# Both token sublayers in a new order: plain x scaled early, x^T's second half split ahead, quadrant sums on VectorE, more low parts by transfers

## The chip, the cores and the metric

The kernel runs on one core of a Trainium2 chip as one program. The metric is the device time of one execution in microseconds: 1684.34, the median of three runs (1683.64 to 1687.1). The engines are named as the profile names them: PE (TensorE's matmuls) and PEld (its weight loads), DVE (VectorE), ACT (ScalarE), POOL (GpSimd) and SP (SyncE, which here only issues transfers).

## The reference

Two layers over 512 tokens of width 1024, in fp32. Each has a token sublayer and a channel sublayer:

```python
for i in range(DEPTH):                       # DEPTH = 2
    proj = x @ w_in[i]
    q_na, k_na, v_na, q_r, k_r, v_r, g_r, gate_a, gate_b = jnp.split(proj, IN_SPLITS, axis=-1)
    ya = neighbourhood_attention(q_na, k_na, v_na, na_rpb[i])          # 8 heads of 64
    yb = bidirectional_retention(q_r, k_r, v_r, g_r, decay_f[i], decay_b[i])   # 4 heads, group norm, silu gate
    merged = sigmoid(gate_a) * (ya @ w_branch_a[i]) + sigmoid(gate_b) * (yb @ w_branch_b[i])
    x = layer_norm(DEEPNORM_ALPHA * x + merged @ w_out[i], ln1_g[i], ln1_b[i])
    ffn = conv_glu_ffn(x, w_up[i], conv_w[i], conv_b[i], w_down[i])
    ple = sigmoid(x @ w_ple_gate[i]) * (p[i] @ w_ple_proj[i])
    x = layer_norm(DEEPNORM_ALPHA * x + ffn + ple, ln2_g[i], ln2_b[i])
```

## The kernel before

**Three products for one.** PE multiplies a reduced-precision type. So each fp32 operand is split in a high part `hi`, a cast by ACT, and a low part `lo = src - hi`, a subtraction by DVE (`split`), and each product is hi*hi + hi*lo + lo*hi in fp32. Weights arrive as 128 x 1024 tiles of 512 KB and are split the same way. A few plain weight tiles are "sent": ACT writes -hi into `lo`, and a transfer issued by POOL accumulates the raw weights onto it out of memory, so that DVE has no part in it (`SENT`, seven tiles).

**Seven products for eight.** The large weight matrices are cut into 2 x 2 quadrants and multiplied in seven block products with the names a, c, t1, d, t2, t3, t4. The t's need sums of quadrants: of weights, by a transfer that accumulates onto a raw tile (rawa, rawt), and of x, on DVE and ACT (`quad_sums`; tiles s, s1, s2). `ON_CHIP` names sums that are instead added on the chip from a tile that is there anyway (the quadrant d, rawd); before, that is block 2's t2 in layer 0, added by POOL. In the token sublayer, blocks 0 to 3 of the input projection (values, gates), and the block 4 (the retention's output projection, "branch b", tiles yw and yq, products u, v, w) are of this kind; heads' q and k (`q0`..`k3`, `nq0`..`nk3`) and the output projection are plain tiles.

**The order.** `Stream` holds all weight tiles in the order of use; `get` prepares (splits) up to `DEEP` items ahead, held to three pairs of hi and lo that lie ready, and loads `LOOK` = 3 further. The order of the token sublayer is a list of names: `VG[l]`, its opening, then `FILL[l]`, between whose items the attention and retention heads are spread at slots (`RET_AT`, `NA_AT`). Side jobs hang on steps of the opening through `at_key` (tables, decay logs, x^T's second half, sums: `TABLES_AT`, `REST_AT`). Then `bb` runs branch b, merges (tiles M, sa), splits the transposed sum (mt), multiplies it by w_out (products gn) and ends with layer norm 1 of `xn`, the plain residual x, tile by tile; `ba` is branch a.

**x of layer 1.** Layer 0's last layer norm leaves its normalised rows R without scale and shift; they are stored to `scr` in memory (L1788, L1815). In layer 1's `bb`, `plain_x` loads them as xn and multiplies by lng and adds lnb (L1126, L1127), four tiles each, on DVE.

**The start.** x^T arrives in two halves of columns (xf, two tiles each), and is split by `first_half` and `second_half`. The second also issues the decay vector `dl` and `zd`, and runs `decay_logs`, the logs of the retention's decay rates, on DVE and ACT. In layer 0's `VG` block 3's a (`3a`) comes first, then `nq0`.

Of the kernel before, what the change touches and what calls it, by code (L numbers as in the profile page):

```python
# [14 lines left out]
P = 128  # L15
# [17 lines left out]
SENT = (('k3', 'q2'), ('k2', 'k3', 'nk2', 'nq3', 'q1'))  # L33
# [4 lines left out]
FILL = (('2c', '3t2', '3d', 'nk1', 'vn', '3t3', '3t4', '2t1', 'nk2', '2t2', '2d', '2t3', '0a', 'nq2', 'k2', '0t1', '2t4', '0t2', '0d', '0t3', '1a', 'q0',  # L38
# [9 lines left out]
OUT_PREP = ((0, 1, 1, 1), (0, 1, 1, 1))  # L48
# [3 lines left out]
VG = (('p0', 'p1', '3a', 'nq0', 'nk3', 'nq3', '3c', '3t1', 'nk0', '2a', 'nq1'), ('3a', '2a', '2c', '3c', '3t1', 'nq0', 'nk1', 'nk0', '3t2'))  # L52

XN_AT = (6, 6)
M_AT = (1, 5)
TABLES_AT = (0, 6)
REST_AT = (1, 1, 1, 1, 7, 8)
PEND_AT = (1, 3)

PG = ("a", "c", "up", "t1", "up", "t2", "up", "d", "up", "t3", "up", "t4")  # L60
PG_HELD = ("t1", "t2", "t3", "t4")
PG_EARLY = "a"
# [14 lines left out]
S_AT = ("up0", "t1", "t2", "up1")  # L77
# [3 lines left out]
VG_EARLY = 'd'  # L81
VG_HELD = (('0c', '0t2', '1a', '1c', '1t2', '1t4', '2a', '2t4', '3t1', '3t2'),
 ('0a', '0c', '0d', '0t3', '1c', '1t4', '2a', '2c', '2t1', '2t3', '3a', '3c', '3d', '3t1', '3t2', '3t3'))
ON_CHIP = (('', '', 't2', ''), ('', '', '', ''))
BB_HELD = (('t2',), ('c', 'd', 't1', 't2', 't4'))
BB_EARLY = ('a', 'a')
RC_ACT = ((0, 2, 3, 5, 6, 7), (3, 4, 6))
# [38 lines left out]
def trunk(tc, wpack, x_nat, x_tr, head, p_tr, rpb, decay, ln_par, ln_col, conv, cos_t, sin_t, dist, xi_d, zd, ident_d, out):  # L126
# [4 lines left out]
    with ExitStack() as es:  # L131
# [49 lines left out]
        class Item:  # L181
# [7 lines left out]
            def __init__(self, kind, src, width, pool=None, plus=None, own=None):  # L189
                self.kind, self.src, self.width, self.pool, self.plus, self.own = kind, src, width, pool, plus, own  # L190
                self.raw = self.hl = None
                self.nxt = self.early = self.block = self.other = None

                self.sent = False

        def block_items(pos, held, early, onchip=""):

            out = []
            prev = {}
            for kind, src, plus in (("a", "a", None), ("c", "c", None), ("t1", None, "b"), ("t2", None, "d"),  # L200
                                    ("d", "d", None), ("t3", "b", "d"), ("t4", None, "c")):
                for j in range(2):
# [6 lines left out]
                    if kind == "t3":  # L209
                        [o for o in out if o.kind == early][j].early = it  # L210
# [1738 lines left out]
```

## Time and profile before

| | before |
|---|---|
| median of three runs | 1684.34 us (1683.64 to 1687.1) |
| the profiled execution | 1689.1 us, its span 1687.3 us |
| mean granted clock of PE | 0.997 |
| bytes read, written | 295.37 MB, 26.21 MB |
| hi casts of one 128 x 1024 tile, ACT | 1.05 us |

The span runs from the first instruction to the last. A row of the timeline gives start, length (us), engine, line, operation, tiles (out<-in), and in brackets the time for which its engine stood idle before it and what released it. Matmuls of PE overlap, so that a row of 0.39 us is followed by the next after 0.23. Where the kernel records instructions and issues them itself in a set order, as in the first 75 us, all of them show the line of that helper, L109. Most of DVE's time is low parts (`lo<-raw,hi` and its kin), most of ACT's is casts.

### The profile page before, as it was taken

The page shows a single profiled execution, that of the slowest core. Times are in us where ns is not written, and L with a number is a line of the kernel's source. Part 1 is how long each engine was busy: PE and PEld are TensorE (multiplying, and loading weights), DVE is VectorE, ACT ScalarE, POOL GpSimd, SP SyncE. Part 2 cuts the span into 40 slices and gives each one's busy share as a digit, 9 for nine tenths or more (in the row PEclk, how much of TensorE's full clock was granted, in tenths as well). Part 3 has the DMA queues.
Part 4 walks back from the last instruction along what each step waited for, and adds up shares of the span by engine and source line. Part 5 has one row for each costly group of instructions (what it writes and reads, how often), then busy time and mean ns, then how long its engine had stood idle before and what let it go on. Part 6 is the DMA issues. An engine that isn't in the chain of part 4 may idle for free.

```text
span 1687.3 us, 22720 instructions
## 1 busy us (share of the span) xinstructions
PE 1656.4 (98%) x8391; PEld 1399.0 (83%) x8391; DVE 1314.1 (78%) x2019; ACT 996.3 (59%) x1520; POOL 232.2 (14%) x277
## 2 busy tenths in 40 slices
PE   8999999999999999999999999999999999999997
PEld 6788888887888889789888888888877888898986
DVE  5847688979687867959976676788897887588598
ACT  5858876635266636546486888464533664474462
POOL 0102101110111111111111011010202111111112
PEclk9999999999999999999999999999999999999999
DMA  8857846556774788697686669544767767787874
GB/s 298 223 169 200 206 98 171 168 161 175 233 208 157 174 272 211 157 258 198 182 239 191 187 163 237 163 100 126 187 205 231 218 180 205 220 202 186 249 194 81
DMA packets 94719, 324.13 MB, mean 192 GB/s; under 512 B 10896, under 2 KB 11408, under 8 KB 94608
## 3 DMA queue, kind: packets, MB, share of 16 engines
q0 software_dynamic: 33840, 121.13, 36.7%
q1 hardware_dynamic: 60768, 201.55, 33.0%
q8 instruction: 66, 1.08, 0.2%
q14 instruction: 45, 0.37, 0.1%
HBM read 295.37 MB, written 26.21 MB: 191 GB/s over the span
## 4 chain that ended last, share of the span: by engine, by line
PE 59%; DVE 14%; issue 13%; DMA 8%; ACT 3%; POOL 1%; SPq 0%; DVEq 0%; POOLq 0%; ACTq 0%
PE u L435 4%; PE u L436 4%; PE u L434 4%; DMA rawa<-in_wpack 4%; PE gt L434 4%; PE gt L435 4%; PE gt L436 4%; PE gt L109 3%; DVE lo L179 3%; PE gn L436 3%; PE gn L434 3%; PE gn L435 3%; PE v L434 3%; PE v L436 3%; PE v L435 3%
## 5 line engine op out<-in xcount | busy, mean ns | idle before, releaser
L179 DVE TENSOR_TENSOR lo<-raw,hi 128x1024 fp32r<-128x1024 f32 (+1 forms) x156 | 188.9, 1217 | 97.6 <-ACT hi L178 97.0
L178 ACT CAST hi<-raw 128x1024 fp32r<-128x1024 f32 (+1 forms) x156 | 161.6, 1045 | 151.1 <-DMA raw<-in_wpack 57.7
L179 DVE TENSOR_TENSOR lo<-rawa,hi 128x1024 fp32r<-128x1024 f32 (+1 forms) x151 | 180.3, 1201 | 64.0 <-ACT hi L178 63.0
L178 ACT CAST hi<-rawa 128x1024 fp32r<-128x1024 f32 (+1 forms) x151 | 154.4, 1032 | 125.9 <-DMA rawa<-in_wpack 49.7
L342 POOL DMA_DIRECT2D rawa<-in_wpack x111 | 98.2, 885 | 624.9 <-DVE lo L179 481.7
L109 PE MATMUL gt<-x1t,hi 128*128 128x512 f32 x384 | 118.3, 389 | 0.0
L434 PE MATMUL gt<-x1t,hi 128*128 128x512 f32 x256 | 99.7, 390 | 0.0
L435 PE MATMUL gt<-x1t,hi 128*128 128x512 f32 x256 | 99.7, 390 | 0.0
L436 PE MATMUL gt<-x1t,lo 128*128 128x512 f32 x256 | 99.6, 389 | 0.0
L434 PE MATMUL gt<-xt,hi 128*128 128x512 f32 x216 | 84.7, 392 | 1.1 <-DVE t L886 0.7
L109 PEld LDWEIGHTS gt<-x1t,hi 128*128 128x128 f32 x384 | 72.1, 188 | 15.0
L435 PE MATMUL gt<-xt,hi 128*128 128x512 f32 x216 | 84.2, 390 | 0.0
L436 PE MATMUL gt<-xt,lo 128*128 128x512 f32 x216 | 84.2, 390 | 0.0
L342 POOL DMA_DIRECT2D rawt<-in_wpack x38 | 33.8, 890 | 309.7 <-DMA rawt<-in_wpack 116.2
L109 PE MATMUL gt<-x1t,lo 128*128 128x512 f32 x192 | 74.9, 390 | 0.1
L109 DVE TENSOR_TENSOR lo<-raw,hi 128x1024 fp32r<-128x1024 f32 (+1 forms) x46 | 54.5, 1197 | 5.2 <-ACT hi L109 4.9
L436 PEld LDWEIGHTS gt<-x1t,lo 128*128 128x128 f32 x256 | 48.1, 188 | 10.1
L434 PEld LDWEIGHTS gt<-x1t,hi 128*128 128x128 f32 x256 | 48.1, 188 | 9.6
L435 PEld LDWEIGHTS gt<-x1t,hi 128*128 128x128 f32 x256 | 48.1, 188 | 9.5
L179 DVE TENSOR_TENSOR lo<-rawt,hi 128x1024 fp32r<-128x1024 f32 (+1 forms) x36 | 42.8, 1193 | 14.8 <-ACT hi L178 14.6
L436 PE MATMUL gn<-hi,mt 128*128 128x512 f32 x128 | 49.3, 391 | 1.5 <-DVE mt L179 1.5
L435 PE MATMUL u<-lo,s 128*128 128x512 f32 x128 | 50.4, 394 | 0.0
(499 smaller groups left out, 5128.6 us busy)
## 6 DMA issues: line engine op xcount, KB each, us to landing
raw<-in_wpack SPq DMA_DIRECT2D x205, 512.0 KB, 4.8
rawa<-in_wpack POOLq DMA_DIRECT2D x124, 512.0 KB, 7.1
rawa<-in_wpack SPq DMA_DIRECT2D x42, 512.0 KB, 6.2
rawt<-in_wpack SPq DMA_DIRECT2D x42, 512.0 KB, 6.0
rawt<-in_wpack POOLq DMA_DIRECT2D x42, 512.0 KB, 7.6
s<-s_scr POOLq DMA_DIRECT2D x32, 512.0 KB, 11.7
s_scr<-s POOLq DMA_DIRECT2D x16, 512.0 KB, 5.1
r_scr<-pp SPq DMA_DIRECT2D x8, 512.0 KB, 10.6
```

What stands on the lines that cost most here:

```text
L109: r = f(*a, **k)
L178: nc.scalar.copy(hi, src)
L179: nc.vector.tensor_sub(lo, src, _f(hi))
L342: nc.gpsimd.dma_start(it.raw[:, :w], wpack[l, c][:, o:o + w], accum_op=ALU.add)
L434: nc.tensor.matmul(ps, lh, rh, start=start, stop=False, skip_group_check=more)
L435: nc.tensor.matmul(ps, lh, rl, start=False, stop=False, skip_group_check=more)
L436: nc.tensor.matmul(ps, ll, rh, start=False, stop=stop, skip_group_check=more)
```

## The change

It reorders both token sublayers' lists and moves six things.

- **x early.** `early_x` multiplies R by lng, adds lnb and stores to `scr` in layer 1's opening (`PX_AT` gives the steps); layer 0's end no longer stores R, and `plain_x` only loads.
- **Start.** `dl` and `zd` are issued behind raw_11; the second half's split runs as a hook within the first `a`, between its product and its copies. The opening of layer 0 is now 3a, 3c, nk1, nq1, 2a, nk3, nq0, 3t1.
- **Quadrant sums.** Blocks 0 and 1 (t2 and t3) in layer 0, block 1's t3 and block 3's t2 in layer 1 and branch b's t2 in both are added by DVE from the raw tile of d (or of the like) when the tile is prepared; POOL adds none.
- **Low parts.** Nine plain tiles in place of seven, both tiles of branch b's d in each layer, and three and one tiles of the output projection are sent: 17 in all.
- **Group norm.** In layer 0 the last scale of the four heads (yb) is done by ACT; more heads' softmax scales (S) are done by DVE (`RC_ACT`).
- The ple projection's stores, tables and sums move to other steps. The switches for the channel sublayer that come with it (`D_CHIP`, `U_CHIP`, `PG_CHIP`, `M_SENT`, `UBP`, `PG_CHORE`) are all off.

```diff
-SENT = (('k3', 'q2'), ('k2', 'k3', 'nk2', 'nq3', 'q1'))
+SENT = (('k0', 'nk2', 'nq2', 'q0', 'q2', 'q3'), ('k2', 'nq1', 'q3'))
...
-FILL = (('2c', '3t2', '3d', 'nk1', 'vn', '3t3', '3t4', '2t1', 'nk2', '2t2', '2d', '2t3', '0a', 'nq2', 'k2', '0t1', '2t4', '0t2', '0d', '0t3', '1a', 'q0',
-  'k0', '0t4', '1t1', '0c', 'k1', 'q1', '1t2', '1d', 'k3', 'q3', '1t3', '1c', 'q2', '1t4', 'ba'),
...
+FILL = (('nk0', 'nq3', '3t2', '3d', 'vn', '3t3', 'nq2', 'nk2', '2c', '3t4', '2t1', '2d', '2t2', '0a', '2t3', '2t4', '0t1', '0t2', '0d', '0t3', 'k2', 'k3',
+  '1a', '0t4', '1t1', '1c', 'k0', '1d', 'k1', 'q0', '1t2', 'q1', '0c', 'q2', '1t3', 'q3', '1t4', 'ba'),
...
-RET_AT = ((33, 32, 38, 37), (31, 38, 36, 39))
-NA_AT = ((10, 13, 13, 16, 18, 19, 20, 23), (6, 9, 9, 10, 11, 11, 17, 20))
+RET_AT = ((36, 36, 38, 40), (37, 39, 38, 40))
+NA_AT = ((9, 9, 13, 14, 15, 19, 21, 24), (7, 8, 10, 12, 13, 14, 20, 21))
...
-VG = (('p0', 'p1', '3a', 'nq0', 'nk3', 'nq3', '3c', '3t1', 'nk0', '2a', 'nq1'), ('3a', '2a', '2c', '3c', '3t1', 'nq0', 'nk1', 'nk0', '3t2'))
+VG = (('p0', 'p1', '3a', '3c', 'nk1', 'nq1', '2a', 'nk3', 'nq0', '3t1'), ('2a', '3a', '3c', 'nq1', 'nq2', '3t1', 'nq0', 'nk1'))
...
+PX_AT = (4, 15, 16, 17, 18, 18, 38, 40, 41, 42)
+GN_ACT = ((0, 1, 2, 3), ())
+BSENT = (('4d',), ('4d',))
+OUT_SENT = ((1, 4, 5), (6,))
...
+BB_CHIP = ('t2', 't2')
...
-ON_CHIP = (('', '', 't2', ''), ('', '', '', ''))
+ON_CHIP = (('t2 t3', 't2 t3', '', ''), ('', 't3', '', 't2'))
...
-RC_ACT = ((0, 2, 3, 5, 6, 7), (3, 4, 6))
+RC_ACT = ((0, 2, 5), (3, 5))
...
             def add(self, it):
                 if it.other is not None:
-                    if it.other.raw is None:
-                        self.fetch(it.other)
-                    nc.gpsimd.tensor_tensor(it.raw, it.raw, it.other.raw, ALU.add)
                     return
...
+                    if it.other is not None:
+                        o = it.other
+                        if o.raw is None:
+                            self.fetch(o)
+                        nc.vector.tensor_add(it.raw[:, :it.width], it.raw[:, :it.width], o.raw[:, :it.width])
...
+        NDL = DEPTH * 8
+        lgs = cp.tile([P, NDL], F32, name="lgs")
+        dl = cp.tile([P, NDL], F32, name="dl_0")
+        nc.sync.dma_start(dl, decay.to_broadcast([P, NDL]))
+        nc.sync.dma_start(zd_sb, zd)
         for kp in range(2):
             x_load(1, kp)
...
             ws.load(11)
-            nc.sync.dma_start(dl, decay.to_broadcast([P, NDL]))
-            nc.sync.dma_start(zd_sb, zd)
...
                         product(kind, st["u"], True)
+                        while hooks:
+                            next(hooks.pop(0))
                         st["p1"] = copies(st["u"], "p1")
...
-                        nc.vector.tensor_scalar_mul(y, y, r[:, i:i + 1])
+                        if h in GN_ACT[l]:
+                            nc.scalar.activation(y, y, AF.Copy, scale=r[:, i:i + 1])
+                        else:
+                            nc.vector.tensor_scalar_mul(y, y, r[:, i:i + 1])
...
                     xn.append(z)
-                    if l:
-                        nc.vector.tensor_mul(z, z, g)
-                        nc.vector.tensor_add(z, z, b)
+
+            def early_x():
+
+                g, b = ln_consts(l - 1, 1)
+                yield
+                for t in range(5):
+                    if t < 4:
+                        nc.vector.tensor_mul(RX[t], RX[t], g)
+                        yield
+                    if t:
+                        nc.sync.dma_start(scr[(t - 1) * P:t * P, :], RX[t - 1])
+                    if t < 4:
+                        nc.vector.tensor_add(RX[t], RX[t], b)
+                    yield
...
                             norm(i)
-                            nc.sync.dma_start(scr[i * P:(i + 1) * P, :], R[i])
```

**SP's queue at the start.** hd is the first product's data, xf the four tiles of x^T, raw and rawa weight tiles, dl the decay vector. Before, from the eighth transfer:

```order
L109 DMA raw_11_123<-in_wpack 128x1024
L109 DMA xf_12_125<-in_x_tr 128x1024
L109 DMA xf_13_127<-in_x_tr 128x1024
L109 DMA raw_24_158<-in_wpack 128x1024
L1698 DMA gb_7332<-in_ln_col 128x16
L109 DMA raw_35_204<-in_wpack 128x1024
L109 DMA cos_sb_88<-in_cos_t 128x512
...
L109 DMA ident_84<-in_ident 128x128
L109 DMA raw_40_249<-in_wpack 128x1024
L109 DMA raw_43_267<-in_wpack 128x1024
L109 DMA dl_0_140<-in_decay 128x16
```

and now:

```order
L125 DMA raw_11_123<-in_wpack 128x1024
L125 DMA dl_0_126<-in_decay 128x16
L125 DMA zd_sb_87<-in_zd 128x4
L125 DMA xf_12_129<-in_x_tr 128x1024
L125 DMA xf_13_131<-in_x_tr 128x1024
L125 DMA raw_26_164<-in_wpack 128x1024
L665 DMA B_115_656<-in_rpb 128x512
L665 DMA B_116_658<-in_rpb 128x512
L125 DMA raw_27_166<-in_wpack 128x1024
```

The decay vector and zd stand ahead of the second half of x^T now, in place of behind the fourteenth large transfer, and the attention's bias tables B between two weight tiles.

**DVE at the start.** lo is a weight tile's low part, xt a split of x^T (xf 12 and 13 are its second half), qn and kl parts of attention heads, p1 a block product's copy. Before:

```order
L109 TENSOR_TENSOR lo_42_264<-raw_24_158,hi_41_263 128x1024
L109 TENSOR_TENSOR xt_0_106<-xf_12_125,xt_0_106 128x2x256
L109 TENSOR_TENSOR xt_0_106<-xf_13_127,xt_0_106 128x2x256
L109 TENSOR_TENSOR xt_0_106<-xf_12_125,xt_0_106 128x2x256
L109 TENSOR_TENSOR xt_0_106<-xf_13_127,xt_0_106 128x2x256
L109 TENSOR_SCALAR dl_1_299<-dl_0_140 128x16
L109 TENSOR_TENSOR dl_1_299<-dl_1_299,dl_0_140 128x16
...
L109 TENSOR_TENSOR lo_48_321<-raw_35_204,hi_47_320 128x1024
L109 TENSOR_TENSOR qn_51_352<-qs_50_349,qn_51_352 64x512 x2
L109 TENSOR_TENSOR lo_53_362<-raw_40_249,hi_52_361 128x1024
```

and now:

```order
L125 TENSOR_TENSOR lo_45_272<-raw_27_166,hi_44_271 128x1024
L125 TENSOR_TENSOR xt_0_106<-xf_12_129,xt_0_106 128x2x256
L125 TENSOR_TENSOR xt_0_106<-xf_13_131,xt_0_106 128x2x256
L125 TENSOR_TENSOR xt_0_106<-xf_12_129,xt_0_106 128x2x256
L125 TENSOR_TENSOR xt_0_106<-xf_13_131,xt_0_106 128x2x256
L125 TENSOR_TENSOR lo_54_310<-raw_38_212,hi_53_309 128x1024
L125 TENSOR_TENSOR lo_56_326<-rawa_43_257,hi_55_325 128x1024
...
L125 TENSOR_TENSOR kl_60_376<-gt_58_350,kn_59_375 64x512 x4
L125 TENSOR_TENSOR lo_62_386<-rawa_46_275,hi_61_385 128x1024
L125 TENSOR_TENSOR qn_65_418<-qs_64_415,qn_65_418 64x512 x2
...
L125 TENSOR_TENSOR s_81_475<-s1_79_472,s_80_474 128x512
L125 TENSOR_SCALAR dl_1_480<-dl_0_126 128x16
```

The decay logs (dl) stood ahead of the sixth weight tile's low part; they now come fifteen rows later, behind the work on the next weight tiles, heads and x's first sums.

**DVE in layer 1, around the merge.** M and sa are the merge, mt the split of its transpose, xn the plain x, lng and lnb the layer norm's scale and shift of the layer before. Before, behind sa:

```order
L1126 TENSOR_TENSOR xn_2013_11366<-xn_2013_11366,lng_2011_11362 128x1024
L1127 TENSOR_TENSOR xn_2013_11366<-xn_2013_11366,lnb_2012_11363 128x1024
L1126 TENSOR_TENSOR xn_2014_11370<-xn_2014_11370,lng_2011_11362 128x1024
L1126 TENSOR_TENSOR xn_2015_11374<-xn_2015_11374,lng_2011_11362 128x1024
L1127 TENSOR_TENSOR xn_2014_11370<-xn_2014_11370,lnb_2012_11363 128x1024
L1127 TENSOR_TENSOR xn_2015_11374<-xn_2015_11374,lnb_2012_11363 128x1024
L1126 TENSOR_TENSOR xn_2016_11378<-xn_2016_11378,lng_2011_11362 128x1024
L179 TENSOR_TENSOR mt_2022_11422<-tr_2020_11416,mt_2021_11421 128x4x128
L1127 TENSOR_TENSOR xn_2016_11378<-xn_2016_11378,lnb_2012_11363 128x1024
L179 TENSOR_TENSOR mt_2022_11422<-tr_2023_11425,mt_2021_11421 128x4x128
L179 TENSOR_TENSOR mt_2026_11438<-tr_2024_11432,mt_2025_11437 128x4x128
L179 TENSOR_TENSOR mt_2026_11438<-tr_2027_11441,mt_2025_11437 128x4x128
```

and now, from sa on:

```order
L1250 TENSOR_TENSOR sa_1868_10606<-sa_1868_10606,M_1987_11259 128x512
L1250 TENSOR_TENSOR sa_1869_10608<-sa_1869_10608,M_1988_11261 128x512
L195 TENSOR_TENSOR mt_2019_11425<-tr_2017_11419,mt_2018_11424 128x4x128
L195 TENSOR_TENSOR mt_2019_11425<-tr_2020_11428,mt_2018_11424 128x4x128
L195 TENSOR_TENSOR mt_2023_11441<-tr_2021_11435,mt_2022_11440 128x4x128
L195 TENSOR_TENSOR mt_2023_11441<-tr_2024_11444,mt_2022_11440 128x4x128
L195 TENSOR_TENSOR lo_2033_11461<-raw_2002_11335,hi_2032_11460 128x1024
L195 TENSOR_TENSOR lo_2035_11465<-raw_2013_11383,hi_2034_11464 128x1024
L195 TENSOR_TENSOR lo_2047_11585<-raw_2016_11401,hi_2046_11584 128x1024
L1366 SCALAR_TENSOR_TENSOR xn_2007_11371<-xn_2007_11371,gn_2038_11472 128x512
L574 BN_STATS bn_2028_11456<-xn_2007_11371 128x6
```

The eight passes over xn are gone from here; they are done on R in layer 1's opening, among the splits kl of the attention's keys:

```order
L1089 TENSOR_TENSOR kl_1426_8187<-gt_1424_8161,kn_1425_8186 64x512
L1192 TENSOR_TENSOR R_783_4293<-R_783_4293,lng_1386_7999 128x1024
L1192 TENSOR_TENSOR R_784_4294<-R_784_4294,lng_1386_7999 128x1024
L1088 TENSOR_TENSOR kl_1426_8187<-gt_1424_8161,kn_1425_8186 64x512
L1089 TENSOR_TENSOR kl_1426_8187<-gt_1424_8161,kn_1425_8186 64x512
L1197 TENSOR_TENSOR R_783_4293<-R_783_4293,lnb_1387_8000 128x1024
L1197 TENSOR_TENSOR R_784_4294<-R_784_4294,lnb_1387_8000 128x1024
L195 TENSOR_TENSOR lo_1432_8243<-raw_1414_8110,hi_1431_8242 128x1024
L772 TENSOR_TENSOR u2_1435_8263<-u2_1435_8263,v_1398_8053 128x512
```

Before, no row of layer 1's opening works on R or xn.

More of the change, by code (lines that the diff above doesn't have):

```diff
@@ L191, in __init__, with block_items @@
                 self.raw = self.hl = None
[L192 to L196 removed]
+                self.nxt = self.block = self.other = None
+                self.early, self.users = [], 0
+                self.sent = self.done = False
+        def block_items(pos, held, early, onchip="", dearly="c"):
             out = []
@@ L232, in down_items @@
                 held.update({k: xp for k in XT_HELD[l]})
-            return block_items(pos, held, "a")
+            out = block_items(pos, held, "a", D_CHIP[s], D_DEARLY)
+            for it in out:
+                it.sent = f"D{s}{it.kind}" in M_SENT
+            return out
         def vg_items(l):
@@ L258, in ub_items @@
                     out += [Item("w", (l, UP0 + 2 * n + i, 0, 1024), 1024) for i in range(2)]
+                    for it in out[-2:]:
+                        it.sent = f"u{n}" in M_SENT
                     n += 1
@@ L366, in load @@
                             self.fetch(it, part)
-                        if it.early is not None:
-                            self.fetch(it.early)
+                        for e in it.early:
+                            if e.raw is None:
+                                self.fetch(e)
                     self.nload += part != 0
@@ L1253, in fillers @@
                 for i, f in enumerate(F):
+                    for g in steps.get(len(keys) + i, ()):
+                        next(g, None)
                     if f == "vn":
@@ L1870, in _pack @@
     su = _stat(w_up)
-    blocks = [2 * sum(SEGS[:s + 1]) - 4 for s in range(3) if UB[s]]
+    blocks = [2 * sum(SEGS[:s + 1]) - 4 for s in range(3) if UB[s] or (UBP and s == 0)]
     for i in range(NF):
```

126 lines of the change are left out of this document (87 added, 39 removed), and 4 rows, old and new, of the table FILL.

## The prediction

> **What bounds the kernel now.** I read first the page's busy times and its DMA queues.
>
> ```profile
> PE 1656.4 (98%) x8391; PEld 1399.0 (83%) x8391; DVE 1314.1 (78%) x2019; ACT 996.3 (59%) x1520; POOL 232.2 (14%) x277
> q0 software_dynamic: 33840, 121.13, 36.7%
> q1 hardware_dynamic: 60768, 201.55, 33.0%
> ```
>
> PE is busy 98% of 1687.3 us, and the change adds and removes no matmul. So only what PE loses while it waits can change: some 31 us of idle time, and what is lost where it runs at half clock. The windows say where to look, and which other engine is full there (columns: the stretch, its length, then busy time and count of PE, PEld, DVE, ACT and POOL, granted clock, DMA share, GB/s).
>
> ```profile
> 0.00:50.00 50.00, 44.15 (x181) 33.30 (x181) 29.18 (x50) 28.47 (x46) 3.48 (x9) 1.00 0.87 287
> 200.00:250.00 50.00, 49.62 (x254) 41.84 (x253) 37.85 (x73) 39.64 (x80) 4.33 (x5) 1.00 0.47 109
> 376.00:392.00 16.00, 14.01 (x59) 11.21 (x58) 15.92 (x23) 10.43 (x15) 3.46 (x4) 0.89 0.73 156
> 398.00:420.00 22.00, 19.95 (x98) 15.90 (x97) 22.00 (x33) 11.23 (x16) 0.00 (x0) 1.00 0.39 144
> 850.00:900.00 50.00, 50.00 (x231) 41.64 (x230) 38.12 (x51) 36.83 (x58) 8.99 (x10) 1.00 0.98 273
> 900.00:950.00 50.00, 50.00 (x224) 41.25 (x223) 28.22 (x43) 36.40 (x60) 1.73 (x2) 1.00 0.53 145
> 1200.00:1250.00 50.00, 47.06 (x222) 37.54 (x221) 49.01 (x66) 31.91 (x47) 4.37 (x5) 1.00 0.72 202
> 1250.00:1300.00 50.00, 46.81 (x218) 38.42 (x217) 40.72 (x53) 11.89 (x23) 9.41 (x8) 1.00 0.76 240
> ```
>
> PE loses in three kinds of place: the first 75 us, where DMA is full and DVE is not; the end of layer 0's token sublayer (376 to 420), where DVE has no gap at all; and the end of layer 1's (1200 to 1300), where DVE is busy 49.01 of 50 us before PE's idle time. In the middle of a sublayer it loses next to nothing: 0.38 us of 200 to 250, none of 850 to 950. The timeline of PE has the single waits; in brackets stand the idle time and what ended it.
>
> ```profile
> 23.50 0.49 PE L109 MATMUL gt<-xt,hi 128*128 128x512 f32 x1 [1.19 <-ACT xt L109]
> 24.22 0.50 PE L109 MATMUL gt<-xt,hi 128*128 128x512 f32 x1 [0.23 <-DVE xt L109]
> ...
> 34.33 0.62 PE L109 MATMUL gt<-xt,hi 128*128 128x512 f32 x2
> ...
> 35.01 0.61 PE L109 MATMUL gt<-xt,hi 128*128 128x512 f32 x2
> 37.84 0.50 PE L109 MATMUL gt<-xt,lo 128*128 128x512 f32 x1 [2.21 <-DVE lo L109]
> ...
> 49.63 0.50 PE L109 MATMUL v<-hi,s 128*128 128x512 f32 x1 [1.02 <-ACT s L109]
> ...
> 72.92 0.50 PE L435 MATMUL w<-lo,xt 128*128 128x512 f32 x1 [0.73 <-DVE lo L109]
> ...
> 387.81 0.66 PE L435 MATMUL u<-lo,yw 128*128 128x512 f32 x1 [2.00 <-DVE lo L179]
> ...
> 415.42 1.26 PE L1134 MATMUL tr<-ident,sa 128*128 128x128 f32 x8 [1.64 <-DVE sa L1179]
> ...
> 1239.13 0.47 PE L434 MATMUL u<-hi,yq 128*128 128x512 f32 x1 [1.17 <-ACT mt L178]
> ...
> 1258.13 0.50 PE L436 MATMUL gn<-hi,mt 128*128 128x512 f32 x1 [1.53 <-DVE mt L179]
> ...
> 1283.65 1.07 PE L1298 MATMUL tr<-ident,xn 128*128 128x128 f32 x8 [1.66 <-DVE xn L509]
> ```
>
> A wait costs about 0.15 us more than its idle time, since the first matmul behind it takes 0.50 us and not 0.39; that is read from these rows alone. One wait cost far more, as the windows of single microseconds behind it show:
>
> ```profile
> 388.00:389.00 1.00, 1.00 (x3) 0.81 (x3) 1.00 (x2) 0.49 (x2) 0.71 (x1) 0.50 0.80 233
> 391.00:392.00 1.00, 1.00 (x5) 0.80 (x4) 1.00 (x3) 0.62 (x1) 0.00 (x0) 0.80 0.93 152
> ```
>
> After the 2.00 us the clock stood at 0.50 from 388 until into the microsecond from 391 (0.80): about 3.4 us at half speed, 1.7 us lost. After the 2.21 us of 37.84 it did not fall (0 to 50 has 1.00). So a wait of 2 us costs 2.2 or 3.9 us. The Trainium skill ("TensorE: Matmul & The Clock Gate", What's actually happening) has the gate fall after an idle window of about 3.4 us; here 2.00 us were enough, so the trace disagrees, and by that rule the wait at 387.81 would be worth only its 2.0.
>
> **The start: x's second half, the decay logs, the first fillers.** Before, the first matmuls behind 3a are nq0's, whose operand is the second half of x^T, still being split (23.50 and 24.22). The wait at 37.84 has another root:
>
> ```profile
> 32.99 0.18 DVE L109 TENSOR_SCALAR dl<-dl 128x16 f32<-128x16 f32 x1 [7.02 <-DMA dl<-in_decay]
> ...
> 36.56 1.22 DVE L109 TENSOR_TENSOR lo<-raw,hi 128x1024 fp32r<-128x1024 f32 x1
> 33.41 0.22 ACT L109 ACTIVATE dl<-dl 128x16 f32<-128x16 f32 x1 [8.41 <-DVE dl L109]
> dl<-in_decay SPq DMA_DIRECT2D x1, 8.0 KB, 10.6
> ```
>
> The decay vector is issued behind fourteen half-megabyte loads and the tables, and takes 10.6 us; DVE stands 7.02 us in front of it and ACT 8.41, its casts behind its exponential. So the lo that PE could use at 35.63 (35.01 + 0.62) starts on DVE at 36.56. The change issues that vector behind the eighth large transfer and puts its DVE work fifteen places later, behind that lo, splits the second half of x^T within the first `a`, and runs 3a and 3c before anything that needs it. The first block order alone puts one whole tile pair of 24 matmuls (24 x 0.227 = 5.4 us; 0.227 is the pace from 34.33 to 35.01, three matmuls in 0.68) between 3a and the first use, against 1.4 us of waiting. So all of 1.34 + 0.38 (the two waits, with 0.15 each) and 2.36 go. The wait at 49.63 is for a quadrant sum that ACT and DVE produce in the same jam, 1.17; I let it go too, since both engines gain 7 to 8 us of lead. The one at 72.92, 0.88, is a c tile's lo, which the new sums do not touch; half. Sum 5.7. Against it: tables B, conv weights and one store now stand in SP's queue ahead of the fourth to sixth weight tile, with DMA 0.87 busy; B and cw are under 1 MB, and 0.5 MB of q1 cost 1.45 us of all 16 queues (33.0% of 1687.3 us by 201.55 MB), so those tiles land up to 3 us later. With three tiles of lookahead that costs 0 to 3; I take 1. **Start: -4.7**, between -1.5 and -6.
>
> **Quadrant sums by VectorE, low parts by transfer.** Sixteen sums that were an accumulating transfer become a DVE add (10 into rawa, 6 into rawt), the two adds by GpSimd among them go; ten low parts more (17 for 7) are made by ACT's negation and an accumulating transfer instead of by DVE. The prices:
>
> ```profile
> L179 DVE TENSOR_TENSOR lo<-raw,hi 128x1024 fp32r<-128x1024 f32 x154 | 187.7, 1224 | 97.6 <-ACT hi L178 97.0
> L393 ACT ACTIVATE lo<-hi 128x1024 fp32r<-128x1024 f32 x7 | 7.4, 1058 | 0.1
> L339 POOL TENSOR_TENSOR rawa<-rawa,rawd 128x1024 f32<-128x1024 f32 x2 | 4.8, 2398 | 42.0 <-DVE lo L179 42.0
> lo<-in_wpack POOLq DMA_DIRECT2D x7, 512.0 KB, 7.5
> ```
>
> DVE: an fp32 add of the same size has no row on DVE but xn+lnb's 1.22, so +16 x 1.22 = 19.5 and -10 x 1.22 = -12.2: +7.3 us over two sublayers of some 430 us each, where DVE has 28 to 44 of 50 us. ACT: +10 x 1.06. DMA: 14 accumulates go with the sums and ten come with the low parts; an accumulate of 512 KB takes 2.68 us of all queues (36.7% of 1687.3 us by 121.13 MB), so -4 x 2.68 = -10.7 us; plain loads stay as they are. In mid-sublayer this is all hidden by the lookahead, as such work is now: 0, between -2 and +2.5 (the new order of fillers is part of this; one wait of 2.2 either way). The sixteen final scales of the group norm that go from DVE to ACT in layer 0 pay for sixteen softmax scales that come the other way; by length they cancel on DVE.
>
> At 376 to 420, where DVE is full, branch b's block is what matters: the two t2 sums come on DVE (+2.4) and are there without the accumulate that ended at 384.86, both d low parts and three of the output projection's go (-2.4 and -3.7). DVE has 3.7 us less, and the wait of 387.81 (2.15 + 1.7 of half clock) is for a lo whose sum came by such a transfer; the one of 415.42 (1.79) keeps its order on both engines. I take one third of the first, **-1.2**, between +2.5 (the output's second low part lands 7.5 us behind its issue and is late) and -3.9.
>
> **Layer 1's end: x scaled early.**
>
> ```profile
> 1246.98 1.23 DVE L1126 TENSOR_TENSOR xn<-xn,lng 128x1024 f32<-128x1024 f32 x1 [0.19 <-DMA xn<-x_scr]
> 1249.38 2.35 DVE L1126 TENSOR_TENSOR xn<-xn,lng 128x1024 f32<-128x1024 f32 x2
> 1255.06 0.68 DVE L179 TENSOR_TENSOR mt<-tr,mt 128x512 fp32r<-128x512 f32 x1
> 1256.79 1.88 DVE L179 TENSOR_TENSOR mt<-tr,mt 128x512 fp32r<-128x512 f32 x3
> ...
> 1277.30 1.23 DVE L179 TENSOR_TENSOR lo<-rawa,hi 128x1024 fp32r<-128x1024 f32 x1
> 1279.04 1.21 DVE L179 TENSOR_TENSOR lo<-raw,hi 128x1024 fp32r<-128x1024 f32 x1
> 1280.17 0.20 DVE L504 BATCH_NORM_AGGREGATE mv<-bn 128x2 f32<-128x12 f32 x1
> ```
>
> Eight passes of 1.14 to 1.26 us stand from 1246.98 to 1256.88 between the merge sa and the last splits of mt, which PE waits for at 1258.13. The change has none there: mt follows sa at once, 9.1 us earlier, so the whole 1.68 goes. Further on two lo's of the MLP stand between xn's last add (1276.59) and its aggregation; in the new order both have gone ahead, since DVE is 9.1 us less behind, and the 2.4 us of them cover the 1.81 of 1283.65. The same lead helps the 1.32 of 1239.13 not at all (it is before); BB_CHIP and sent d work there as in layer 0, -0.5. **Layer 1's end: -4.0**, between -2 and -5.3. The eight passes now stand near 900 us, among the kl splits: DVE has 21.8 us free from 900 to 950, 11.9 from 850 to 900. Price 0; were that cover gone, 9.1 us in one piece against three tiles' lookahead cost up to 3. The four stores of x move from layer 0's end into that stretch, 4 x 1.45 us of DMA that is 0.98 busy from 850 and 0.53 from 900: also covered.
>
> **Sum.** -4.7 + 0 - 1.2 - 4.0 = -9.9: 1689.1 becomes 1679.2. The profiled execution is 4.8 us above the runs' median of 1684.34, so I expect **1674.5**.
>
> **Rivals.**
> (1) The low parts come late and the kernel is slower. A low part by DVE is there 1.2 us behind its cast; one by transfer 1.06 + 0.9 (issue) + 7.5 = 9.5 us. A tile in a block feeds 12 matmuls, 2.7 us of PE, so three tiles' lookahead is 8.2 us: from a lead under 9.5 us on, PE waits, here 1.3 us and 0.15 for each, and 1.7 more where the clock falls. Ten new ones at 1.45 and five falls: 23 us, 1697 with the gains kept; at half as many late and the start's gain lost too, 1691. Against it: the list of PE's waits before names no transfer of a low part, with seven of them. The Trainium skill ("DMA: Bandwidth & Descriptors", Issuing engines are not separate DMA queues) lets transfers of every engine interleave on the same 16 queues, which speaks for it where DMA is at 0.98; no run here has shown such a wait. 0.11.
> (2) The waits only move: in branch b DVE stays full, the start is bound by DMA (0.87) and a later tile is late instead. Only the layer 1 end is then won, and half of that given back in the changed middle: -2, 1682. 0.15.
> (3) The change gains more: the waits of 387.81 and 1239.13 go whole (-3.9 - 1.3 against -1.7 taken), the start loses nothing (-1), and of the middle's small waits (0.38 in 50 us, over some 560 us: 4) half go: 1668. 0.14.
> (4) The forecast, 1671 to 1680: 0.60.
>
> **How the numbers follow.** A difference under 0.2%, 3.4 us, can't be told from none. Faster than 1681.0: the forecast, the third rival and a third of the second, 0.79; within: 0.10; slower than 1687.7: 0.11. The range 1666 to 1687 leaves out the first rival and the ends of the third and the second.
>
> **What would show it.** Right: no wait before 45 us over 0.5; dl's first DVE operation without a wait for a transfer; mt splits right behind sa in layer 1 and no wait of PE at mt or xn there; eight passes over R near 890 us with PE still full. Wrong: a wait of PE for a lo that a transfer ends; PE's idle time in the start unchanged with raw tiles as its releaser; clock of 0.50 behind new waits; DVE without a gap and PE waiting between 850 and 950.

## The result and the profile after

| | before | changed |
|---|---|---|
| median of four runs | 1685.72 us (1683.64 to 1687.17) | 1669.13 us (1666.95 to 1670.38) |
| ratio, 95% interval | | 0.9905 (0.9891 to 0.9918) |
| the profiled execution, its span | 1689.1, 1687.3 us | 1666.95, 1665.2 us |

The change is worth 16.6 us between the medians. The two profiled executions lie 22.1 us apart, since that of before is slower than its four runs and that of the changed kernel the fastest of its own; what follows on places is read from these two, and its sum is 22.1.

The page of the changed kernel, its span, busy times and DMA queues:

```profile
span 1665.2 us, 22737 instructions
PE 1648.3 (99%) x8391; PEld 1399.5 (84%) x8391; DVE 1318.7 (79%) x2025; ACT 1005.7 (60%) x1530; POOL 221.8 (13%) x271
q0 software_dynamic: 33264, 119.03, 35.6%
q1 hardware_dynamic: 60768, 201.55, 33.5%
```

PE's idle time is the span less its busy time: 1687.3 - 1656.4 = 30.9 before, 1665.2 - 1648.3 = 16.9 now, 14.0 less. Its busy time for the same 8391 matmuls is 8.1 us less too. A list of waits does not show these 8.1. Some 4.5 of them go with 17 waits fewer (26 over 0.15 us before, 9 now): the first matmul behind a wait takes 0.50 us, where one in a row adds 0.23. Another 1.7 are the half clock behind 387.81, 3.4 us long, which the changed kernel does not have between 10 and 1640 us. The rest is spread. DVE has 4.6 us more to do and is still not the loss; q0's accumulating transfers are only four fewer.

The same windows as before the change, shifted only where the work moved (columns as there):

```profile
0.00:50.00 50.00, 48.80 (x207) 38.45 (x208) 31.87 (x46) 35.36 (x53) 5.33 (x11) 1.00 0.97 325
50.00:100.00 50.00, 50.00 (x222) 41.40 (x221) 35.70 (x56) 40.58 (x63) 5.18 (x6) 1.00 0.78 212
350.00:400.00 50.00, 48.54 (x228) 39.01 (x228) 46.78 (x73) 32.73 (x46) 6.62 (x8) 1.00 0.70 184
850.00:900.00 50.00, 50.00 (x222) 41.42 (x221) 42.93 (x53) 34.04 (x53) 5.12 (x6) 1.00 0.72 207
900.00:950.00 50.00, 49.85 (x238) 41.39 (x238) 37.08 (x69) 37.43 (x71) 0.93 (x2) 1.00 0.60 186
1200.00:1250.00 50.00, 48.21 (x226) 39.42 (x225) 42.13 (x57) 25.99 (x35) 3.45 (x4) 1.00 0.70 203
1250.00:1300.00 50.00, 50.00 (x238) 41.79 (x237) 39.75 (x56) 24.77 (x43) 12.49 (x12) 1.00 0.77 218
```

The first 50 us have PE busy 48.80 in place of 44.15, though DMA is fuller (0.97 for 0.87). Layer 1's end (1200 to 1250) has DVE at 42 in place of 49 us. DVE's eight early passes stand in 850 to 950, which PE hardly feels (0.15 idle). The list of PE's waits (engine, tile and line that waited, for what; us in all, times, longest) has shrunk from 22 rows to seven:

```profile
PE tr L1205 <- DVE sa L1250: 2.2, 2, 1.6
PE warm L597 <- DVE warm L594: 1.2, 1, 1.2
PE v L490 <- ACT yw L859: 1.1, 1, 1.1
PE v L490 <- DVE R L1773: 0.8, 2, 0.4
PE v L492 <- DVE yw L862: 0.5, 1, 0.5
PE u L492 <- DVE yw L862: 0.5, 1, 0.5
PE tr L1205 <- issue: 0.3, 1, 0.3
```

No wait for x^T, for a weight's low part, for mt or for xn is left; none is for a transfer. The largest is the merge sa of layer 1, 1.64 us, which had been 0.51 there: a part of what was won behind it is given back ahead of it. In layer 0's branch b and merge four waits are left, 1.9 us together, where before there were three of 4.0 us (387.81, 400.52 and 415.42):

```profile
368.23 0.50 PE L492 MATMUL v<-hi,yw 128*128 128x512 f32 x1 [0.53 <-DVE yw L862]
377.26 1.23 PE L1205 MATMUL tr<-ident,sa 128*128 128x128 f32 x8 [0.31 <-issue]
379.03 0.50 PE L492 MATMUL u<-hi,yw 128*128 128x512 f32 x1 [0.53 <-DVE yw L862]
402.51 1.26 PE L1205 MATMUL tr<-ident,sa 128*128 128x128 f32 x8 [0.51 <-DVE sa L1250]
```

### The profile page after: what moved, and what is told of

It reads as the page before. It is cut to its first block, busy times and chain, and to the rows that moved or that the text cites. A ratio compares the mean times of both kernels' runs of the same rounds, so it can differ in the third digit from the quotient of the medians.

```text
span 1665.2 us, 22737 instructions
## 1 busy us (share of the span) xinstructions
PE 1648.3 (99%) x8391; PEld 1399.5 (84%) x8391; DVE 1318.7 (79%) x2025; ACT 1005.7 (60%) x1530; POOL 221.8 (13%) x271
## 4 chain that ended last, share of the span: by engine, by line
PE 85%; DVE 9%; ACT 2%; DMA 2%; issue 2%; POOL 0%; DVEq 0%; ACTq 0%; POOLq 0%
PE gt L125 9%; PE gt L490 6%; PE gt L491 6%; PE u L492 6%; PE u L490 6%; PE gt L492 6%; PE u L491 6%; PE v L490 4%; PE u L125 4%; PE v L492 4%; PE v L491 4%; PE gn L490 4%; PE gn L491 4%; PE gn L492 4%; DVE lo L195 2%
## 5 line engine op out<-in xcount | busy, mean ns | idle before, releaser
L195 DVE TENSOR_TENSOR lo<-raw,hi 128x1024 fp32r<-128x1024 f32 (+1 forms) x142 | 171.0, 1212 | 88.4 <-ACT hi L194 87.8
L194 ACT CAST hi<-raw 128x1024 fp32r<-128x1024 f32 (+1 forms) x142 | 147.1, 1044 | 111.7 <-PE gt L491 39.7
L386 POOL DMA_DIRECT2D rawa<-in_wpack x103 | 90.2, 882 | 570.3 <-DVE lo L195 456.4
L490 PE MATMUL gt<-xt,hi 128*128 128x512 f32 x224 | 87.7, 391 | 0.0
L491 PE MATMUL gt<-xt,hi 128*128 128x512 f32 x224 | 87.2, 389 | 0.0
L125 DVE TENSOR_TENSOR lo<-raw,hi 128x1024 fp32r<-128x1024 f32 (+1 forms) x44 | 52.1, 1196 | 6.4 <-ACT hi L125 6.3
L386 POOL DMA_DIRECT2D rawt<-in_wpack x32 | 28.8, 922 | 211.0 <-DMA rawt<-in_wpack 136.3
L490 PE MATMUL u<-hi,s 128*128 128x512 f32 x128 | 50.1, 392 | 0.0
```

What stands on the lines that cost most here:

```text
L125: r = f(*a, **k)
L194: nc.scalar.copy(hi, src)
L195: nc.vector.tensor_sub(lo, src, _f(hi))
L386: nc.gpsimd.dma_start(it.raw[:, :w], wpack[l, c][:, o:o + w], accum_op=ALU.add)
L490: nc.tensor.matmul(ps, lh, rh, start=start, stop=False, skip_group_check=more)
L491: nc.tensor.matmul(ps, lh, rl, start=False, stop=False, skip_group_check=more)
```

## The experiments

Names that begin with b are the kernel before with one piece of the change, names with a the changed kernel with one piece undone. Each ratio is to the kernel before, run beside it; the changed kernel's own is 0.9905. 0.001 is 1.7 us.

**The decay vector alone (b_dl).**

```diff
+        nc.sync.dma_start(dl, decay.to_broadcast([P, NDL]))
+        nc.sync.dma_start(zd_sb, zd)
         for kp in range(2):
             x_load(1, kp)
...
-            nc.sync.dma_start(dl, decay.to_broadcast([P, NDL]))
-            nc.sync.dma_start(zd_sb, zd)
```

> The kernel before with one edit: the decay vector and zd are issued behind the eighth large transfer (raw_11) and not behind the fourteenth. Theory (the late decay vector holds DVE and ACT, and with them the low part that PE waits for at 37.84): the first dl operation on DVE waits for no transfer, the wait of 2.2 us at PE is gone, and probably the one of 1.0 at 49.6 too: 2.4 to 3.6 us less than before, about 1682.5. The waits at 23.5 and 24.2 stay. Rival (the start is bound by its weight transfers, DMA busy 0.87): the wait stays with the raw tile's arrival as its root, 0 to 0.5 us less.

Measured: 0.9991 (0.9979 to 1.0003), not told from no change in time; the mechanism is plain in DVE's timeline of this kernel.

```profile
25.45 0.17 DVE L109 TENSOR_SCALAR dl<-dl 128x16 f32<-128x16 f32 x1
...
29.02 1.22 DVE L109 TENSOR_TENSOR lo<-raw,hi 128x1024 fp32r<-128x1024 f32 x1
```

The dl work waits for nothing, and the low part that began at 36.56 begins at 29.02; PE's waits of 2.21 and 1.02 are gone, those at 23 us stay (1.19 and 0.23). So the cause was named rightly. In the same execution layer 1's end is worse: its wait for mt is 2.36 and brings the half clock, where before it was 1.53 without.

**Early x alone (b_earlyx).** Scale, shift and store in layer 1's opening at the same steps as in the change; all else as before.

```diff
-                        nc.vector.tensor_mul(z, z, g)
-                        nc.vector.tensor_add(z, z, b)
...
+                px = early_x()
+                for i in PX_AT:
+                    at_key(i, px)
```

> The kernel before with one edit: R is scaled, shifted and stored in layer 1's opening, plain x is only loaded, layer 0's end stores nothing. Theory (eight passes of 1.14 us between sa and the last mt are what PE waits for): the waits of 1.5 at 1258 and 1.7 at 1284 are gone and PE loses nothing near 890 to 950: 3.5 us less, about 1682. Rival A (DVE is full to the end anyway and the next low part is late in place of mt): at most 1 us less. Rival B (the passes stand in the way where they are now): new waits of PE in layer 1's opening of 1 to 3 us, net 0.

Measured: 1.0006 (0.9997 to 1.0015). The two waits at the end are gone, as in the theory; rival B took it all back. PE's timeline in layer 1's opening, and ACT's:

```profile
911.27 0.51 PE L435 MATMUL v<-hi,s 128*128 128x512 f32 x1 [0.64 <-ACT hi L179]
912.72 0.50 PE L436 MATMUL v<-lo,s 128*128 128x512 f32 x1 [0.95 <-DVE lo L180]
...
926.92 0.50 PE L437 MATMUL gt<-xt,lo 128*128 128x512 f32 x1 [2.75 <-DMA lo<-in_wpack]
```

```profile
909.22 1.99 ACT L179 CAST hi<-raw 128x1024 fp32r<-128x1024 f32 x2 [6.83 <-DMA raw<-in_wpack]
```

In the old order of layer 1's opening ACT stands 6.8 us for a raw tile at 909, and behind that a sent low part is issued late and lands at 927. The raw tile itself was issued at 901.30, right behind a low part of DVE that ended at 901.24; DVE was busy 9.87 of the 10 us from 890 to 900 there, with three passes just ahead (887.66 to 891.25), and 7.04 in the kernel before. Three waits of 4.3 us together, against 0.14 us there in the changed kernel. What covers early x in the changed kernel is its new order and its new choice of sent tiles together; no run parts the two, and with the old choice in the new order a wait of 2.54 us for a sent low part is back near the same place (a_fillsent, 901.36).

**Early x undone (a_latex).** The reverse of that edit on the changed kernel.

> The changed kernel with early x undone: plain x is scaled and shifted on DVE behind its load, as before, and R is stored in layer 0's end. Theory (the early passes bring the gain at layer 1's end by themselves): both waits come back, 3.5 us more than the changed kernel, about 1672.6. Rival (the sent low parts alone free DVE there): 0 to 1 us more.

Measured: 0.9919 (0.9904 to 0.9934), 1673.78 us; by the ratios 2.4 us more than the changed kernel, by the medians 4.7. The intervals of the two ratios overlap, so the size is not settled. In the trace one of the two waits came back, and with the half clock; the other (xn) is 0.24 us. PE's timeline and the windows of single microseconds:

```profile
1243.68 0.60 PE L492 MATMUL gn<-hi,mt 128*128 128x512 f32 x1 [2.28 <-DVE mt L195]
```

```profile
1244.00:1245.00 1.00, 1.00 (x4) 0.73 (x3) 1.00 (x2) 0.00 (x0) 0.00 (x0) 0.50 0.00 0
1246.00:1247.00 1.00, 1.00 (x3) 0.78 (x3) 1.00 (x2) 0.00 (x0) 0.00 (x0) 0.50 0.61 184
```

**The opening's order (a_nq0first) and the hook (a_nohook).**

```diff
-VG = (('p0', 'p1', '3a', '3c', 'nk1', 'nq1', '2a', 'nk3', 'nq0', '3t1'),
+VG = (('p0', 'p1', '3a', 'nq0', 'nk1', 'nk3', '3c', '3t1', '2a', 'nq1'),
```

> The changed kernel with layer 0's opening in an order like the old one: 3a, nq0, nk1, nk3, 3c, 3t1, 2a, nq1, so that the second half of x^T is used right behind 3a; the decay vector stays early and the split stays a hook within the first a. Theory (the order of the opening buys the 5.4 us that the second half's split needs): PE waits 1.3 to 2 us near 23 us again, 1.5 to 3 us more than the changed kernel. Rival (the hook alone brings the split in time): no wait there, within 0.5 us.

```diff
-HOOK = (1, 1)
+HOOK = (0, 1)
```

> The changed kernel with the split of x^T's second half no longer a hook within the first a: it comes at the step before nk1, behind 3c. Order of the opening and the early decay vector stay. Theory (the order gives the lead, the hook is spare): a wait of PE of 1 to 2 us at the first use of the second half, since the split then stands right in front of it: 1 to 2 us more. Rival (the hook is not needed): within 0.5 us.

Measured: 0.9967 (0.9954 to 0.9980) and 0.9963 (0.9949 to 0.9978); each loses some 10 us of the 16, far more than expected. Without the hook PE waits once, for 8.14 us, at the first use of the second half; ACT's timeline of that kernel tells why.

```profile
25.05 1.05 ACT L125 CAST hi<-raw 128x1024 fp32r<-128x1024 f32 x1 [1.13 <-DMA raw<-in_wpack]
31.84 1.04 ACT L125 CAST hi<-rawa 128x1024 fp32r<-128x1024 f32 x1 [5.74 <-DMA rawa<-in_wpack]
32.91 1.28 ACT L125 ACT_TABLE_LOAD   x1
34.78 1.23 ACT L125 ACTIVATE p<-p 128x512 f32<-128x512 f32 x2 [0.59 <-DVE p L125]
35.91 2.16 ACT L125 CAST xt<-xf 128x512 fp32r<-128x512 f32 x4
```

The split of x^T (last row) has had its data for long. It stands behind a cast that waits 5.74 us for a weight tile, a table load and two activations. In the changed kernel the split runs at 23.73 and the same cast, which waits 2.32 there at 30.14, keeps nobody waiting. With nq0 first PE waits 1.75 and 0.84 at the old place (24.54 and 25.88), with half clock from 26.98 on, and then 2.86 at 54.93 for a cast of ACT that stands behind one for a sum of x, which waited 2.17 for DVE:

```profile
54.93 0.80 PE L125 MATMUL v<-hi,s 128*128 128x512 f32 x1 [2.86 <-ACT hi L125]
```

Its row is 0.80 long, not 0.50: the clock was at half from 54.28 on, for 6.8 us. In both kernels the cast that PE waits for is held up by one that stands ahead of it in ACT's queue; in a_nohook that one waits for a transfer, here for a sum.

**The start alone on the kernel before (b_start).** Decay vector, hook, and the old items in the new order; the decay logs and the tables' second step at the later steps.

> The kernel before with the start alone made new: decay vector early, the split of the second half as a hook within the first a, opening 3a, 3c, nk0, nq1, 2a, nk3, nq0, 3t1, nq3 (the old items in the new order), tables' second step and decay logs at later steps. Sums, low parts and early x stay as before. Theory (the start's gain is the opening's own): PE's loss in the first 100 us falls from 7.8 to under 1.5, 6 to 7 us less than before, ratio 0.996. Rival (the start needs the on-chip sums too, since accumulating transfers load the queues there): 2 to 4 us less, with a wait for a rawa tile behind 40 us.

Measured: 0.9981 (0.9970 to 0.9991), 3 us less. In the first 100 us one wait over 0.5 is left, 1.23 at 55.7 for a sum of x, where the kernel before has 5.4 us of waits (by the windows its PE stands still 6.6 us there, 1.2 of them ahead of its first matmul, and not the 7.8 that I expected to fall). So the new start by itself takes about 4 us of waits away, and the kernel loses part of it at layer 1's end (the wait for mt is 2.02 here, with the half clock). The size is the rival's, but its wait for a rawa tile is not seen.

**The sums (a_dmasum, a_bbdma).** All sixteen sums back to accumulating transfers, and only branch b's.

```diff
-ON_CHIP = (('t2 t3', 't2 t3', '', ''), ('', 't3', '', 't2'))
+ON_CHIP = (('', '', '', ''), ('', '', '', ''))
...
-BB_CHIP = ('t2', 't2')
+BB_CHIP = ('', '')
```

> The changed kernel with all sixteen quadrant sums on the chip undone: rawa and rawt get their second summand by an accumulating transfer again. Theory (sums on DVE matter where the accumulate is late: branch b of both layers and the start, where DMA is 0.97 busy): 2 to 5 us more than the changed kernel, ratio to the kernel before 0.992 to 0.9935, with waits of PE for a t2 low part in branch b. Rival (lookahead hides the transfer; a sum on DVE costs 1.2 us of a full engine): within 1 us of the changed kernel or faster.

> The changed kernel with only branch b's two t2 sums back on accumulating transfers (BB_CHIP off in both layers). Theory (the wait of 387.8 came by this transfer): a wait of about 2 us for a t2 low part comes back in layer 0's branch b, with about 3.4 us at half clock behind it, and the like in layer 1: 2 to 6 us more. Rival (DVE has now lead enough through the sent low parts, whatever the sum is made by): within 1 us.

Measured: 0.9996 (0.9984 to 1.0008), the whole gain gone, and 0.9945 (0.9927 to 0.9963), 6.7 us of it. The first shows in layer 0's filler part, in PE's and ACT's timelines:

```profile
204.62 0.80 PE L490 MATMUL u<-hi,s 128*128 128x512 f32 x1 [4.06 <-ACT u L766]
```

```profile
202.91 1.04 ACT L194 CAST hi<-rawt 128x1024 fp32r<-128x1024 f32 x1 [9.51 <-DMA rawt<-in_wpack]
203.98 1.07 ACT L766 COPY u<-u 128x512 f32<-128x512 f32 x2
```

PE waits for a copy by ACT of its own last product, and that copy stands behind a cast that waits 9.51 us for a summed tile. I had looked for waits for low parts; the tile is late, and ACT's queue hands the delay on to whoever is behind. In a_bbdma the wait of 387.8 does not come back. In layer 0 two others appear, 1.13 and 0.94 for ACT near 392, again behind a cast that waits, 6.03 us, for a summed tile (388.50). In layer 1 a sent low part is late, in a_dmasum too (2.72 at 1227.10). First the wait in a_bbdma, then the transfers of branch b's two sent low parts in layer 1, in a_bbdma and in the changed kernel (last column: us from issue to landing, their median):

```profile
1219.19 0.50 PE L491 MATMUL v<-lo,yq 128*128 128x512 f32 x1 [2.52 <-DMA lo<-in_wpack]
```

```profile
lo<-in_wpack POOLq DMA_DIRECT2D x2, 512.0 KB, 10.2
```

```profile
lo<-in_wpack POOLq DMA_DIRECT2D x2, 512.0 KB, 6.4
```

The same transfers land after 10.2 us among the accumulates of the sums and after 6.4 without; in layer 0 it is 11.4 and 7.1. The sums on VectorE are what makes room for the sent low parts.

**Sums by transfer and d's low part by VectorE (a_bbdma_dvd).** As a_bbdma, with `BSENT = ((), ())`.

> The changed kernel with branch b's t2 sums back on accumulating transfers and d's low parts back on DVE; the output projection's sent low parts stay. It stands beside a_bbdma, in which d's low part came by a transfer, landed 10 us after its issue and kept PE waiting 2.5 us in layer 1. Theory (the transfers of sums and of low parts delay each other): no wait of PE for a low part's transfer there, so in layer 1's branch b 1.5 to 3 us less than a_bbdma, about 1676. Rival (DVE's two more low parts cost as much as the transfer's delay): within 1 us of a_bbdma, 1678, with waits for DVE instead.

Measured: 0.9922 (0.9909 to 0.9936), 3.9 us less than a_bbdma by the ratios. No wait in branch b is put down to a low part's transfer any more, as the theory has it. Layer 0 has another wait in its place:

```profile
379.78 1.23 PE L1205 MATMUL tr<-ident,sa 128*128 128x128 f32 x8 [2.08 <-issue]
```

DVE writes that sa at 378.99, behind a low part that waits 2.17 us for ACT, whose cast waits 2.17 for a summed tile. With sums and d's low parts both by the new ways the ratio is 0.9905, with neither 0.9922 (these two intervals overlap), and with the low parts sent but the sums by transfer 0.9945: where the sums still go by transfer, sending d's low parts costs time.

**The sent low parts (a_bbnosent, a_fillsent, a_out145).**

```diff
-BSENT = (('4d',), ('4d',))
-OUT_SENT = ((1, 4, 5), (6,))
+BSENT = ((), ())
+OUT_SENT = ((), ())
```

> The changed kernel with the eight sent low parts of branch b's d and of the output projection back on DVE; the sums stay on DVE. Theory (DVE is full there, each low part is 1.2 us of it): waits of PE in branch b and at sa of 1 to 3 us more in layer 0 (five low parts, 6 us of DVE), 0.5 to 1.5 in layer 1 (three): 2 to 4 us more. Rival (the sums on DVE are what counts): within 1 us.

Measured: 0.9932 (0.9913 to 0.9950), 4.5 us more than the changed kernel. DVE is the bound there: in layer 0 it has no gap from 362 to 381, and PE waits 1.37 at 370 and 1.04 at 378; in layer 1 a second wait for sa comes up (1.48 at 1228.4).

```diff
-SENT = (('k0', 'nk2', 'nq2', 'q0', 'q2', 'q3'), ('k2', 'nq1', 'q3'))
+SENT = (('k3', 'q2'), ('k2', 'k3', 'nk2', 'nq3', 'q1'))
```

> The changed kernel with the plain tiles' sent low parts chosen as before (seven in place of nine, other tiles); branch b's and the output's stay sent. Theory (in mid-sublayer the lookahead covers either way): within 1.5 us of the changed kernel, ratio 0.990 to 0.9915. Rival (the choice of tiles is what frees DVE in front of the heads): 2 to 4 us more, with waits of PE for DVE between 150 and 350.

Measured: 0.9947 (0.9932 to 0.9962), 7 us more. Neither theory nor rival: PE waits for no DVE there but twice for the low part's transfer itself. PE's timeline, and two of the microseconds behind the first wait:

```profile
901.36 0.50 PE L492 MATMUL gt<-xt,lo 128*128 128x512 f32 x1 [2.54 <-DMA lo<-in_wpack]
...
1093.29 0.50 PE L492 MATMUL gt<-xt,lo 128*128 128x512 f32 x1 [2.81 <-DMA lo<-in_wpack]
```

```profile
903.00:904.00 1.00, 1.00 (x4) 0.81 (x3) 0.97 (x2) 0.00 (x0) 0.00 (x0) 0.50 1.05 266
905.00:906.00 1.00, 1.00 (x4) 0.80 (x3) 0.00 (x0) 0.00 (x0) 0.00 (x0) 0.50 1.07 279
```

Two waits of 5.35 us together and 1.7 us for the half clock behind each more than account for the 7 us. The choice of tiles to send belongs to the order: the old choice in the new order costs that much.

The last tries to go on from the changed kernel: layer 1's output sent as in layer 0, against its wait of 1.64 at sa.

```diff
-OUT_SENT = ((1, 4, 5), (6,))
+OUT_SENT = ((1, 4, 5), (1, 4, 5))
```

> The changed kernel with three low parts of layer 1's output projection sent (1, 4 and 5, as in layer 0) in place of one (6). In the changed kernel two low parts of 1.14 us stand ahead of the last M and sa, for which PE waits 1.64 us at 1229. Theory (DVE is the bound there): that wait falls to about 0.5, as in layer 0, 1 us less than the changed kernel, ratio about 0.990. Rival (the low parts land too late, or ACT's negations push the mt casts): a new wait, 0 to 3 us more.

Measured: 0.9962 (0.9950 to 0.9974), 10 us worse than the changed kernel. Both came true, the theory first and the rival with more than I had given it:

```profile
1231.94 1.26 PE L1205 MATMUL tr<-ident,sa 128*128 128x128 f32 x8 [0.51 <-DVE sa L1250]
...
1242.72 0.80 PE L491 MATMUL gn<-lo,mt 128*128 128x512 f32 x1 [7.90 <-DMA lo<-in_wpack]
```

The wait for sa fell from 1.64 to 0.51, and the next low part landed 12.1 us behind its issue. No version tried beats the changed kernel.

## Why the prediction was right, and where it was short

The time, 1669.1, lies in the range of 1666 to 1687; the forecast case (1671 to 1680) and its 1674.5 gave 9.9 us where 16.6 came. The third rival, that the change gains more, is the nearest, 1668. Matmul for matmul, the profile of the changed kernel is 12.9 us ahead at layer 0's last transpose of sa, where the sum has 5.9 (start, middle, branch b); 14.7 at the end of layer 0; 17.3 at layer 1's last transpose of sa; and 21.0 at the last of xn there, so that layer 1's end brings 3.7 from sa on.

- **Start, -4.7.** Mechanism right in each part: b_dl takes away the two waits put down to the decay vector, a_nq0first brings back the two put down to the order. The gross 5.7 was about what the waits held (5.4 idle). The 1 us set against it, for weight tiles behind tables and a store, did not come: ACT does wait for a late tile at 30.14, and PE has other work.
- **Middle, 0.** Too small: PE's small waits in it (0.38 at 236.6, 0.69 at 1137.8 and their like) are mostly gone; how much of it is the sums and how much the order was not told apart, since undoing the sums alone brings a new wait of 4.06 that neither kernel has.
- **Layer 0's branch b, -1.2.** This term was mis-sized. I took one third of the wait of 387.81 with its half clock; all of it went, and the wait for sa fell from 1.64 to 0.51. Three small new waits, 1.4 us together, take some of it back. I had written that the order of sa is the same on both engines and kept its wait; DVE came there earlier, though. I had also put the wait of 387.81 down to a sum that came by a transfer; the runs do not bear that out, since with the sums back on transfers (a_bbdma) it stays away, and with the low parts back on DVE (a_bbnosent) too. The last wait for sa stays at 0.51 to 0.52 in both. So which piece took these two away stays open.
- **Layer 1's end, -4.0.** Waits of 6.1 us before, 2.9 now from the first yw to the last xn: 3.2, and some tenths behind each. About right in size; a_latex brings mt's wait back. The price of 0 for the early passes came true by luck: it rested on the free time of DVE before the change, and b_earlyx, with just this free time, loses it all. What made it true is the rest of the change, its order and its choice of sent tiles, which I had not credited with it.
- **The price of a wait.** I priced all but one at 0.15 us beyond their idle time, from rows of 0.50 in place of 0.39. But a matmul in a row adds only 0.23, so that a wait costs some 0.27 more than its idle time. The wait of 1.02 shows it: without it the matmul at 49.63 would have started 0.23 behind the one at 48.23, at 48.46, and the next follows it after 0.34. With the half clock that makes most of the 8.1 us of busy time that went, of 22.1 us between the profiles.
- **The first rival** (late low parts, 0.11) did not happen in the changed kernel, and its mechanism is real: a_fillsent, a_bbdma, a_dmasum, a_out145 and b_earlyx each show PE waiting 2.5 to 7.9 us for one. My point from which it decides, a landing of 9.5 us against 8.2 of lookahead, does not part them: those waited for landed 6.4 to 12.1 us behind their issue, and in the changed kernel two landings of 10.3 and 10.8 us kept nobody waiting. When the transfer is issued counts as much. The Trainium skill ("DMA: Bandwidth & Descriptors", Issuing engines are not separate DMA queues) says that transfers of all issuers share the 16 engines and interleave; a_bbdma agrees, 10.2 us against 6.4 for the same two transfers beside more or fewer accumulates.

That the pieces undone one at a time cost 2.4 to 15.3 us each, together far more than the 16 of the whole, and that three of them alone give -3.2, -1.5 and +1 us (the last two not told from nothing), is shown by the runs: the gain is that of pieces fitted to one another. Which steps of the list of fillers carry it was not tried. Nor were the scales that ACT and DVE exchange (`GN_ACT`, `RC_ACT`) or the switches that say which tiles are held and when the raw tiles for the sums are loaded (`VG_HELD`, `VG_EARLY`, `BB_HELD`, `BB_EARLY`), which changed as well.

## What to carry to other kernels

Where one engine is 98% busy, ask of each of its waits not only what is late but what stands ahead of the late thing in its own engine's queue: a cast in front of it that waits for a transfer passes that wait on to all behind, and here a split moved ahead of it was worth a wait of 8 us. A low part, a sum or any operand made by a transfer needs 5 to 12 us of lead here, by what else the queues carry; move such work off a full engine only where the lead is there, and take other transfers away at the same place. Test a piece of a tuned order alone before crediting it: of three pieces tried alone here, one was worth 3 us and two nothing that can be told from zero.

## What the runs showed of the hardware

Waits of PE cost more than their length. In the fourteen profiles, between 10 and 1640 us, PE stood still for 0.94 to 1.70 us 44 times, and the clock stayed at 1.00 behind each. It stood still 17 times for 1.75 to 2.86 us, and behind 13 of these the granted clock was at 0.50, for about 3.4 us behind 12 of them, which costs 1.7 us; after the four others (2.08, 2.21, 2.52, 2.75) it was not. Three longer ones (4.06, 7.90, 8.14) all brought it. The rule of the Trainium skill cited ahead of the result ("TensorE: Matmul & The Clock Gate", What's actually happening) puts the limit at an idle window of some 3.4 us; in these runs less was enough.

What decides can be read from the clock records of the same traces. In each profile all changes of the clock lie whole steps of 3.413 us apart, within 0.003 us; in the kernel before, for one, at 387.99, 391.41 and 1681.65, which is 1 and 378 steps. The first change to full clock comes 4.25 to 7.11 us into the span, though PE's first matmul starts at 1.19 or 1.20 in all fourteen, so the steps do not start with the kernel. Cut into such steps, the fourteen profiles show, between 10 and 1640 us, no half clock behind any step at full clock in which PE stood still for 1.79 us or less in all, and half clock behind all 16 steps with 1.81 us or more. The four waits that kept the clock were cut in two by the end of a step: 2.21 into 0.80 and 1.42, 2.08 into 0.73 and 1.35, 2.52 into 0.73 and 1.79, 2.75 into 1.68 and 1.07. The 1.75 brought the half clock because 0.84 more followed in the same step, 1.81 in all. The 2.00 at 387.81 lay whole in one step.

By these numbers a wait of 2 us that lies in one step would gain some 2 us, not 0.4, if it were cut to 1.6; a single wait of up to 1.7 us never lowered the clock; and where the steps lie is not set by the kernel's start.
